# Gating and last rows on VectorE, a second PSUM bank for the scan's transposes, and decays and pool products written at other places

## The chip, the cores and the metric

The kernel runs on one core of a Trainium2 chip. Five engines work side by side, each through its own instructions in order: TensorE (PE; its weight loads are shown as PEld), VectorE (DVE), ScalarE (ACT), GpSimd (POOL) and SyncE (SP), which here only issues DMA transfers. ACT and POOL issue DMAs too, in line with their other work. [...] The metric is the device time of one execution in microseconds, the median of several runs.

## The reference

One layer over 512 latent tokens (and 256 context tokens as a prefix), 1024 wide, all in fp32:

```python
u = rmsnorm(h, g) * (1 + scale) + shift          # adaLN; shift, scale, gate from silu(c) @ ada_w + ada_b
z, xbc, dt, pool, q, k, v = split(u @ w_in)      # one input projection
y = ssd(xbc, dt, forward) + ssd(xbc, dt, backward) + d_skip * xs
ssd_out = rmsnorm(y * silu(z), ssd_norm_g)       # gate, then norm
pool_out = (window means of pool - pool) @ pool_w * pool_scale
na_out = neighbourhood attention(q, k, v, context k and v)
h = h + g1 * (concat(ssd_out, pool_out, na_out) @ w_out)
u = rmsnorm(h, norm2_g) * (1 + sc2) + sh2
h = h + g2 * peer_ffn(u)                         # 8 heads, 128 x 128 product keys, top 16 each
out = rmsnorm(h, final_g)
```

The SSD scan works in chunks of 128 tokens. Its decays are exponentials of sums of `dt * a` inside a chunk: to the chunk's end (en), over the whole chunk (to) and from its start (in), each for the forward and the backward direction. The expert part takes, for every token, 128 of 16384 experts; each expert is a row of `peer_u` and a row of `peer_v`.

## The kernel before

Matmuls of the large projections are done in three passes: an operand x is split into a rounded part (ACT copies it, line 175) and a remainder (mostly DVE subtracts, line 178), and `mm3` (lines 185 to 187) adds high times high, high times low and low times high. So each weight block needs a DMA on SP's queue, a copy on ACT and a subtraction on DVE before PE can use it. Weight blocks go through a few buffers (`ws`), so a block is split when PE has left the block that had its buffer.

The order of work comes from two sources. Inside `tc.manual_schedule()` every engine (or the engines that it names) takes its instructions in the order in which the program writes them. Elsewhere a planner orders the instructions of each engine, by the program's order and its own estimate of when operands are ready; `tc.keep_in_program_order` binds the instruction that it wraps. In both cases an engine that waits for an operand holds up all that is queued behind it on that engine.

The stages, in order:

1. *Input projection* (from about 20 to 232 us, planned from line 430 on). `projT` computes a block of 128 columns for all tokens into banks of `psG` (six). For the SSD columns (`cb` 0 to 11) a convolution and transposes follow. Between the projections the generator `ada_rest` is advanced by `next(ada)`, 17 times in all: it works out the second and third of three banks of the modulation. Each advance loads two 128 x 1024 pieces of `ada_w` and adds them, weighted, into `adac` on DVE (lines 478 and 480); after eight of them, at the ninth and at the seventeenth advance, line 484 sums `adac` over partitions on PE, line 487 adds the bias, line 489 stores the rows on SP's queue and line 492 transposes them. Then come four pool blocks: a projection, sums over windows on POOL (lines 626 to 633), and a 128 x 128 matmul in `pool_out` (line 613), which is put off by two blocks, so that the last two stand in the first two of four K projections. The V projection for the context follows.
2. *Scan* (to about 407, manual). A plan of 61 steps (`at(step, f, ...)`) lists what is issued in each; the same steps carry the projections of z, of V and of q (`z_mm`, `q_mm`) as other work for PE. PSUM: `psT` one bank, `psM` two, `psY` one, `psG2` four. Six `decay` calls stand ahead of the plan. For each chunk c the outputs are gathered in `ys[c]`: `o_add` multiplies on DVE and adds on POOL (lines 881 and 882), then `f_gate` multiplies by silu(z) on POOL (line 906), `f_square` squares on ACT, `f_norm` scales on DVE, `f_T` transposes 512 columns into the bank of `psT` (line 924), `f_out` empties it on DVE with the norm's gain (line 930), and `f_store` writes to `mix_d`. `f_T` and `f_out` occur twice for each chunk, one step apart.
3. *Attention and first half of the output projection* (to about 505, manual).
4. *Output projection and second norm* (to about 580; PE in program order, other engines planned in the first part). `out_end` scales an accumulator on DVE (line 1232), adds it to h (POOL for the first half, line 1233) and squares on ACT (line 1234); its buffer `otmp` has two copies. Two operations on `bcr` (lines 1247 and 1248, POOL) work out a gain row that the second norm of row block 3 reads.
5. *Queries, top 16 and routing* (to about 820) *and dense routing weights* (to about 1060).
6. *Experts* (to 1790). 128 steps; in each, a block of 128 experts' `peer_u` and `peer_v` for row blocks 0 to 2; row block 3 is done by gathering rows, in `accG`. The last three steps' `peer_v` products run by row block (`e_v(P - a, t)`), so that a row block can be ended while PE works on the next.
7. *The end.* For each row block: `f_mul` multiplies by the gate row and adds h (lines 1802 and 1803), `f_gain` multiplies by the final norm's gain (line 1815), `f_sq` squares on ACT, and `f_norm` takes the root and scales, half on ACT and half on DVE, or all on ACT. Additions and gains of row blocks 3, 0 and 1 run on POOL, those of 2 on DVE.

Of the kernel before, what the change touches and what calls it, by code (L numbers as in the profile page):

```python
# [148 lines left out]
def build(tc, A, out, dbg=None):  # L149
# [129 lines left out]
    an = si.tile([P, 2, NT, NH], F32, name="an")  # L279

# [185 lines left out]
    def ada_bank(bank, pool):  # L466

        adab = pool.tile([P, 512], F32, name="adab")
        nc.scalar.dma_start(adab, A["ada_b"][:, (bank - 1) * 512:bank * 512])
        part = pool.tile([P, 2048], F32, name="adac")  # L470
        for k in range(KB):
            n = (bank - 1) * KB + k
            for jj in range(2):
                w = xin[(2 * n + jj) % NT] if n < 12 else xin[3 + (2 * n + jj) % 3]
                nc.sync.dma_start(w, A["ada_w"][k * P:(k + 1) * P, (bank - 1) * 2048 + jj * 1024:(bank - 1) * 2048 + (jj + 1) * 1024])
                dst, ck = part[:, jj * 1024:(jj + 1) * 1024], cc[:, k, 0:1]
                if k:
                    tc.keep_in_program_order(V.scalar_tensor_tensor(dst, w, ck, dst, ALU.mult, ALU.add))
                else:
                    tc.keep_in_program_order(V.tensor_scalar(dst, w, ck, None, ALU.mult))  # L480
            yield None
# [6 lines left out]
        for j in range(4):  # L488
            nc.sync.dma_start(mod_d[bank - 1, j:j + 1, :], m[32 * j:32 * j + 1, :])
        pt = psT.tile([P, 4, P], F32, name="pt")  # L490
        for q in range(4):
            PE.transpose(pt[:, q, :], m[:, q * P:(q + 1) * P], ident)

        yield pt.rearrange("p m (j r) -> p j m r", r=32)

    def ada_rest():

        for r in ada_bank(1, ad1):
            if r is None:
                yield  # L500
            else:
                V.tensor_copy(jm(sh2T), r[:, 2:4, :, 0])
        for r in ada_bank(2, ad1):
            if r is None:
                yield
            else:
                V.scalar_tensor_tensor(jm(sc2T), r[:, 0:2, :, 0], 1.0, jm(n2g), ALU.add, ALU.mult)
# [131 lines left out]
    for b in range(4):  # L639
# [4 lines left out]
        if pend:  # L644
            pool_out(*pend.pop(0))
    tc.keep_in_program_order(S.activation(pl1.tile([P, 1], F32, name="warmx"), epsc, AF.Exp))
    accs = projC(V0)
    for t, acc in enumerate(accs):
        V.tensor_copy(vc[:, t, :], acc)
# [75 lines left out]
    for i in range(16):  # L725
        at(fs(4 * i), p_load, i + 2)
        at(fs(4 * i + 1), p_split, i + 1)
        for t in range(4):
            if i < 12:
                if i + t:  # L730
                    at(fs(4 * i + t), z_mm, i // 4, i % 4, t)
# [9 lines left out]

    af = an[:, 0].rearrange("p t h -> p (t h)")
    ab = an[:, 1].rearrange("p t h -> p (t h)")
    HC = NT * NH

    def decay(mask, mov, nm):
        ps = psM.tile([P, 512], F32, name="mm")
        PE.matmul(ps[:, :HC], mask, mov, start=True, stop=True)
        d = m1.tile([P, NT, NH], F32, name=nm)
        S.activation(d.rearrange("p t h -> p (t h)"), ps[:, :HC], AF.Exp)  # L750
        return d
    enF, enB = decay(SU, af, "enF"), decay(SL, ab, "enB")
    z_mm(0, 0, 0)
    toF, toB = decay(ONE, af, "toF"), decay(ONE, ab, "toB")
    inF, inB = decay(U_in, af, "inF"), decay(L_in, ab, "inB")
    V.tensor_tensor(enB, enB, dtn[:, 1], ALU.mult)
    V.tensor_tensor(enF, enF, dtn[:, 0], ALU.mult)
# [143 lines left out]
    def f_gate(c):  # L901
        if "yraw" in dbg:
            nc.sync.dma_start(dbg["yraw"][c * P:(c + 1) * P, :], ys[c])
        for g in range(2):
            gs, hs = half_of(g)
            G.tensor_tensor(ys[c][:, gs], ys[c][:, gs], zts[c, g], ALU.mult)
# [930 lines left out]
    with order:  # L1837
# [6 lines left out]
        for i in range(-6, P + 1):  # L1844
# [23 lines left out]
            if i == 64:  # L1868
                f_load()
            if i == P - 6:  # L1870
                h_load()
# [60 lines left out]
```

## Time and profile before

| | us |
|---|---|
| median of 3 runs (lowest, highest) | 1805.65 (1803.29, 1807.18) |
| the profiled execution | 1804.08 |
| its span, first to last instruction | 1802.0 |
| first decay matmul (scan) | 232.56 |
| first attention scores | 407.58 |
| last matmul starts | 1789.55 |

The span is what the trace shows; the profiled execution took 2.1 us more around it. In a timeline's row stand the start, the duration, the engine, the line of the program, the operation, its output and inputs by name, the shapes and the count; in brackets how long the engine had been idle and what it had waited for. "ACTq" and "SPq" are DMAs issued by ACT and SP. Several instructions of one line in direct sequence are merged into one row, whose duration is that of all.

### The profile page before, as it was taken

To read this page: it belongs to the slowest core of one execution; us is meant where nothing else is said; L and a number is where in the kernel's file an instruction comes from. 1 tells how busy PE (TensorE), PEld (TensorE's weight loads), DVE (VectorE), ACT (ScalarE), POOL (GpSimd) and SP (SyncE) were. 2 spreads that over 40 slices of the span, in tenths; PEclk is the share of its full clock that TensorE was granted. 3 is DMA by queue.
4 is the path that set the end of the run, shared out by engine and by line. 5 is a ranking of instruction groups with operands and counts; after the bars stand their busy time and mean duration, and the time that the engine had idled before them with its cause. 6 is when DMAs were issued, how large, how long until landed. Compare 5 with 4: busy or idle time off the path is not lost.

```text
span 1802.0 us, 26025 instructions
## 1 busy us (share of the span) xinstructions
PE 1755.1 (97%) x9527; PEld 1497.4 (83%) x9527; DVE 1400.1 (78%) x2606; ACT 842.8 (47%) x1497; POOL 406.2 (23%) x276
## 2 busy tenths in 40 slices
PE   6999999999999999999999999999999999999996
PEld 4787776666678889999999998888888888888885
DVE  5679467966635579898999978878878888888876
ACT  4433255456535333456677764434434444444443
POOL 1103410352224443310111121211111111111103
PEclk9999999999999999999999999999999999999999
DMA  9347432168333533576999989999999999999971
GB/s 358 104 144 253 146 90 65 57 211 274 111 106 118 172 112 116 156 266 218 342 342 345 354 307 398 403 353 340 362 344 349 338 396 348 360 349 339 371 242 49
DMA packets 192048, 455.40 MB, mean 253 GB/s; under 512 B 13704, under 2 KB 117384, under 8 KB 173968
## 3 DMA queue, kind: packets, MB, share of 16 engines
q1 hardware_dynamic: 147280, 259.79, 42.6%
q0 software_dynamic: 18576, 136.32, 19.8%
q10 hardware_dynamic: 26064, 57.62, 8.7%
q8 instruction: 75, 1.23, 0.3%
q14 instruction: 53, 0.43, 0.1%
HBM read 401.10 MB, written 54.67 MB: 253 GB/s over the span
## 4 chain that ended last, share of the span: by engine, by line
PE 80%; DVE 2%; ACT 2%; issue 1%; DMA 1%; POOL 1%; SPq 0%; ACTq 0%; POOLq 0%; DVEq 0%
PE pu L185 10%; PE pu L187 10%; PE pu L186 10%; PE pv L186 9%; PE pv L187 9%; PE pv L185 9%; PE acc L185 4%; PE acc L187 4%; PE acc L186 4%; PE mm L845 2%; PE gdps L1651 1%; PE gdps L1652 1%; PE sps L1047 1%; PE mm L787 1%; PE pt L1077 1%
## 5 line engine op out<-in xcount | busy, mean ns | idle before, releaser
L178 DVE TENSOR_TENSOR wl<-wraw,wh 128x1024 fp32r<-128x1024 f32 x294 | 368.1, 1264 | 110.2 <-ACT wh L175 108.1
L175 ACT ACTIVATE wh<-wraw 128x1024 fp32r<-128x1024 f32 x328 | 341.2, 1053 | 196.9 <-PE acc L186 70.7
L185 PE MATMUL pu<-u2h,wh 128*128 128x384 f32 x1024 | 349.7, 342 | 0.0
L186 PE MATMUL pu<-u2l,wh 128*128 128x384 f32 x1024 | 344.8, 337 | 0.8 <-DVE u2l L178 0.8
L187 PE MATMUL pu<-u2h,wl 128*128 128x384 f32 x1024 | 345.4, 337 | 0.0
L1590 POOL DMA_INDIRECT row<-in_peer_uv,idxG x128 | 156.6, 1223 | 804.8 <-DVE accG L1604 710.8
L186 PE MATMUL pv<-wl,wwh 128*128 128x512 f32 x768 | 300.7, 392 | 1.9 <-DVE wl L178 1.8
L185 PE MATMUL pv<-wh,wwh 128*128 128x512 f32 x768 | 301.2, 392 | 0.3 <-ACT wh L175 0.3
L187 PE MATMUL pv<-wh,wwl 128*128 128x512 f32 x768 | 300.9, 392 | 0.0
L186 PEld LDWEIGHTS pu<-u2l,wh 128*128 128x128 f32 x1024 | 192.5, 188 | 2.9 <-DVE u2l L178 1.1
L185 PEld LDWEIGHTS pu<-u2h,wh 128*128 128x128 f32 x1024 | 192.3, 188 | 1.8
L187 PEld LDWEIGHTS pu<-u2h,wl 128*128 128x128 f32 x1024 | 192.2, 188 | 0.7 <-DVE wl L178 0.6
L186 PEld LDWEIGHTS pv<-wl,wwh 128*128 128x128 f32 x768 | 144.2, 188 | 33.6 <-DVE wl L178 3.5
L187 PEld LDWEIGHTS pv<-wh,wwl 128*128 128x128 f32 x768 | 144.2, 188 | 32.2
L185 PEld LDWEIGHTS pv<-wh,wwh 128*128 128x128 f32 x768 | 144.3, 188 | 30.4 <-ACT wh L175 0.7
L1604 DVE SCALAR_TENSOR_TENSOR accG<-row,wG,accG 128x1024 f32<-128x1024 f32 x127 | 162.5, 1280 | 4.7 <-ACT wG L1599 3.4
L1595 DVE CUSTOM_DVE_ANT_0 row<-row,u2G 128x1024 f32<-128x1024 f32 x128 | 155.2, 1219 | 0.0
L175 ACT ACTIVATE wwh<-acl 128x384 fp32r<-128x384 f32 x86 | 45.2, 526 | 206.4 <-DVE acl L1763 134.3
L1654 ACT ACTIVATE stg<-gdps 128x512 f32<-128x512 f32 x96 | 101.5, 1170 | 19.7 <-PE gdps L1652 17.2
L178 POOL TENSOR_TENSOR wl<-wraw,wh 128x1024 fp32r<-128x1024 f32 x34 | 81.6, 2405 | 112.1 <-ACT wh L175 80.5
L1757 ACT ACTIVATE act<-pu 128x384 f32<-128x384 f32 x42 | 20.6, 491 | 162.0 <-PE pu L187 147.9
L1763 DVE TENSOR_TENSOR act<-act,gd 128x384 f32<-128x384 f32 x42 | 23.5, 559 | 87.0 <-ACT act L1757 87.0
(410 smaller groups left out, 3113.1 us busy)
## 6 DMA issues: line engine op xcount, KB each, us to landing
wraw<-in_peer_ut SPq DMA_DIRECT2D x128, 512.0 KB
wraw<-in_peer_uv SPq DMA_DIRECT2D x128, 512.0 KB
gd<-gd_d SPq DMA_DIRECT2D x15, 1536.0 KB
gd_d<-stg ACTq DMA_DIRECT2D x11, 2048.0 KB
wraw<-in_w_in SPq DMA_DIRECT2D x40, 512.0 KB
acl<-act_d SPq DMA_DIRECT2D x86, 192.0 KB
act_d<-act ACTq DMA_DIRECT2D x84, 192.0 KB
wraw<-in_w_out SPq DMA_DIRECT2D x16, 512.0 KB
```

Of the source, the lines that this page charges most:

```text
L175: S.activation(hi, full, AF.Copy)
L178: (eng or V).tensor_tensor(lo, full, hi.bitcast(F32), ALU.subtract)
L185: PE.matmul(ps, ah, bh, start=start, stop=False)
L186: PE.matmul(ps, ah, bl, start=False, stop=False)
L187: PE.matmul(ps, al, bh, start=False, stop=stop)
L845: PE.matmul(ps, m, ms[d].rearrange("p a b -> p (a b)"), start=d == 0, stop=d == 1)
L1590: G.indirect_dma_start(out=rows[k], out_offset=None, in_=A["peer_uv"], in_offset=bass.IndirectOffsetOnAxis(ap=idxG[:, k:k + 1], axis=0))
L1595: V.tensor_tensor_reduce(row[:, 0:D], row[:, 0:D], u2G, 1.0, 0.0, ALU.mult, ALU.add, actG[:, k:k + 1])
L1604: V.scalar_tensor_tensor(accG, row[:, D:2 * D], wG[:, k:k + 1], accG, ALU.mult, ALU.add)
L1654: S.activation(stg[:, :, t0:t0 + 4].rearrange("p a t -> p t a"), ps, AF.Copy, scale=1.0 / GSCALE)
L1757: S.activation(ac[a], pu[:, :TD], AF.Gelu)
L1763: V.tensor_tensor(xq, xq, gds.pop(a), ALU.mult)
```

## The change

- The six decay tiles are allocated with the scan's inputs. Their matmuls and exponentials, bound to program order, stand between the K and the V projections, in two banks of `psG`; the products with `dtn` follow them. The `z_mm(0, 0, 0)` that stood between them is in the plan's step 0. An exponential that only loaded ACT's table (`warmx`) is left out.
- The generator is cut into `ada_sum` (one load-and-add), `ada_row` (lines 484 to 489) and `ada_col` (the transposes and what follows). Bank 1's row comes with the tenth advance, its transposes with the eleventh; bank 2's with the seventeenth and an eighteenth, after the V projection's matmuls. `adac` has two buffers.
- `pool_out` for the last two pool blocks stands after the second and the third K projection, instead of after the first and the second.
- `f_gate` multiplies on DVE.
- `f_T` writes its second half (`q4` 1) into `psY`'s bank.
- The two `bcr` operations are bound to program order.
- The end: h is loaded two steps earlier for row block 3; all additions run on DVE; there is no `f_gain`: `f_norm` is one fused DVE operation per half, (h times 1/rms) times gain, and each half is stored by SP and by ACT. Roots and reciprocals are issued apart. Row block 0's last products come one group earlier.

```diff
-        for k in range(KB):
-            n = (bank - 1) * KB + k
...
+    def ada_rest():
+        for n in range(16):
+            ada_sum(1 + n // KB, n % KB)
+            if n == 9:
+                ada_row(1)
+            if n == 10:
+                ada_col(1)
+            yield
+        ada_row(2)
+        yield
+        ada_col(2)
...
-        if pend:
+        if b and pend:
             pool_out(*pend.pop(0))
...
-    tc.keep_in_program_order(S.activation(pl1.tile([P, 1], F32, name="warmx"), epsc, AF.Exp))
+    HC = NT * NH
+    def decays(specs):
+        ps = psG.tile([P, 512], F32, name="acc")
+        for i, (mask, d, _) in enumerate(specs):
+            tc.keep_in_program_order(PE.matmul(ps[:, i * HC:(i + 1) * HC], mask, an[:, d].rearrange("p t h -> p (t h)"), start=True, stop=True))
+        for i, (_, _, t) in enumerate(specs):
+            tc.keep_in_program_order(S.activation(t.rearrange("p t h -> p (t h)"), ps[:, i * HC:(i + 1) * HC], AF.Exp))
+    decays([(SU, 0, enF), (SL, 1, enB), (ONE, 0, toF)])
+    decays([(ONE, 1, toB), (U_in, 0, inF), (L_in, 1, inB)])
+    for t, d in ((enB, 1), (enF, 0)):
+        V.tensor_tensor(t, t, dtn[:, d], ALU.mult)
     accs = projC(V0)
+    next(ada, None)
...
-            G.tensor_tensor(ys[c][:, gs], ys[c][:, gs], zts[c, g], ALU.mult)
+            V.tensor_tensor(ys[c][:, gs], ys[c][:, gs], zts[c, g], ALU.mult)
...
-        pt = psT.tile([P, 4, P], F32, name="pt")
+        pt = psY.tile([P, 512], F32, name="yd").rearrange("p (a b) -> p a b", a=4) if q4 else psT.tile([P, 4, P], F32, name="pt")
...
-            G.tensor_tensor(bcr, bcr, n2row, ALU.mult)
-            G.tensor_tensor(bcr, bcr, n2row, ALU.add)
+            tc.keep_in_program_order(G.tensor_tensor(bcr, bcr, n2row, ALU.mult))
+            tc.keep_in_program_order(G.tensor_tensor(bcr, bcr, n2row, ALU.add))
...
-        (V if t == 2 else G).tensor_tensor(hx[t][:, hs], sq[:, hs], hx[t][:, hs], ALU.add)
+        V.tensor_tensor(hx[t][:, hs], sq[:, hs], hx[t][:, hs], ALU.add)
...
     def f_norm(t):
         y = sqs[t][:, D:2 * D]
+        for hf in range(2):
+            hs = slice(hf * 512, (hf + 1) * 512)
+            V.scalar_tensor_tensor(y[:, hs], hx[t][:, hs], fss[t][:, 1:2], fgr[:, hs], ALU.mult, ALU.mult)
+            (nc.sync, nc.scalar)[hf].dma_start(out[t * P:(t + 1) * P, hs], y[:, hs])
...
-        for a, t in ((3, 0), (2, 0), (3, 1), (1, 0), (2, 1), (1, 1)):
+        for a, t in ((3, 0), (2, 0), (1, 0), (3, 1), (2, 1), (1, 1)):
             e_v(P - a, t)
             if a == 1:
                 f_mul(t, 0)
+                f_sq(t, 0)
                 f_mul(t, 1)
+                f_sq(t, 1)
+                if t == 0:
+                    f_rec(3)
+                    f_norm(3)
                 else:
-                    f_norm(3)
+                    f_rstd(0)
         for hf in range(2):
             for a in range(P - 3, P):
                 e_v(a, 2, (hf,))
+            f_mul(2, hf)
+            f_sq(2, hf)
+            f_rec(0) if hf == 0 else f_rstd(1)
         f_norm(0)
+        f_rec(1)
+        f_rstd(2)
+        f_norm(1)
+        f_rec(2)
         f_norm(2)
```

More of the change, by code (lines that the diff above doesn't have):

```diff
@@ L279, in build @@
     an = si.tile([P, 2, NT, NH], F32, name="an")
+    enF, enB, toF, toB, inF, inB = (si.tile([P, NT, NH], F32, name=nm) for nm in ("enF", "enB", "toF", "toB", "inF", "inB"))
     gp = Pools()
@@ L464, in build, with ada_sum, ada_row @@
     ad1 = adp.sb("ad1")
-    def ada_bank(bank, pool):
-        adab = pool.tile([P, 512], F32, name="adab")
-        nc.scalar.dma_start(adab, A["ada_b"][:, (bank - 1) * 512:bank * 512])
-        part = pool.tile([P, 2048], F32, name="adac")
-        for k in range(KB):
-            n = (bank - 1) * KB + k
[L473 to L481, printed above, removed]
+    adac = {}
+    def ada_sum(bank, k):
+        if k == 0:
+            adac[bank] = ad1.tile([P, 2048], F32, name="adac", bufs=2)
+        part = adac[bank]
+        n = (bank - 1) * KB + k
+        for jj in range(2):
+            w = xin[(2 * n + jj) % NT] if n < 12 else xin[3 + (2 * n + jj) % 3]
+            nc.sync.dma_start(w, A["ada_w"][k * P:(k + 1) * P, (bank - 1) * 2048 + jj * 1024:(bank - 1) * 2048 + (jj + 1) * 1024])
+            dst, ck = part[:, jj * 1024:(jj + 1) * 1024], cc[:, k, 0:1]
+            if k:
+                tc.keep_in_program_order(V.scalar_tensor_tensor(dst, w, ck, dst, ALU.mult, ALU.add))
+            else:
+                tc.keep_in_program_order(V.tensor_scalar(dst, w, ck, None, ALU.mult))
+    def ada_row(bank):
+        adab = ad1.tile([P, 512], F32, name="adab")
+        nc.scalar.dma_start(adab, A["ada_b"][:, (bank - 1) * 512:bank * 512])
+        part = adac.pop(bank)
         ps = psG.tile([P, 512], F32, name="acc")
@@ L729, in build @@
             if i < 12:
-                if i + t:
-                    at(fs(4 * i + t), z_mm, i // 4, i % 4, t)
+                at(fs(4 * i + t), z_mm, i // 4, i % 4, t)
                 if i % 4 == 3:
@@ L740, in build @@
                        v_d.rearrange("(r c) d -> r c d", c=64)[:, KCOL[g]:KCOL[g] + 32, :]))
[L742 to L757, printed above, removed]
     def hbc(ap):
@@ L1780, in f_load, with h_load @@
         row_bc(g2r, 2, 2, nc.sync)
-    hx = {}
-    def h_load():
-        hr = gls[1].tile([P, NQ, 8 * TQ], F32, name="gd", bufs=2).rearrange("p q t -> p (q t)")
-        for t in (3, 0, 1, 2):
+    hx, stds = {}, {}
+    def h_load(ts):
+        if 3 not in ts:
+            hr = gls[1].tile([P, NQ, 8 * TQ], F32, name="gd", bufs=2).rearrange("p q t -> p (q t)")
+        for t in ts:
             hx[t] = u2G if t == 3 else hr[:, t * D:(t + 1) * D]
```

64 lines of the change are left out of this document (17 added, 47 removed).

## The prediction

> **What bounds the kernel now.** I read the page's first lines, then the table of stretches, then what TensorE (PE) waited for, then the timelines around those waits.
>
> ```profile
> span 1802.0 us, 26025 instructions
> PE 1755.1 (97%) x9527; PEld 1497.4 (83%) x9527; DVE 1400.1 (78%) x2606; ACT 842.8 (47%) x1497; POOL 406.2 (23%) x276
> ```
>
> PE is busy 97%: an edit can win only what PE stands idle, what it runs at half clock, and the end after its last matmul. The stretches (us, then PE, PEld, DVE, ACT, POOL busy with counts, granted clock, DMA share, GB/s) show where these lie:
>
> ```profile
> 147.00:197.00 50.00, 46.85 (x219) 35.65 (x220) 48.82 (x36) 13.39 (x20) 31.66 (x24) 1.00 0.84 269
> 384.70:387.80 3.10, 0.00 (x0) 0.00 (x0) 2.52 (x5) 1.52 (x5) 0.95 (x2) 1.00 0.51 184
> 387.80:391.20 3.40, 3.36 (x8) 2.25 (x9) 1.77 (x5) 0.29 (x1) 0.71 (x1) 0.50 0.16 48
> 580.00:1770.00 1190.00, 1189.61 (x6551) 1073.34 (x6550) 995.57 (x1965) 564.23 (x925) 239.42 (x166) 1.00 0.84 304
> ```
>
> From 580 to 1770 PE idles 0.4 us, so whatever is won ahead of 580 arrives at the end undiminished. Near the scan's end PE stands still for 3.1 us and then runs 3.4 us at clock 0.50. The waits of PE (total, times, longest), the last row from the stretch 1770 to 1802:
>
> ```profile
> PE pt L924 <- DVE y L930: 3.2, 1, 3.2
> PE acc L484 <- DVE adac L478: 2.2, 1, 2.2
> PE acc L185 <- DVE otmp L1232: 1.7, 1, 1.7
> PE acc L613 <- POOL pa L633: 1.5, 1, 1.5
> PE acc L613 <- POOL pb L633: 0.9, 1, 0.9
> PE pv L186 <- DVE wl L178: 1.5, 2, 0.8
> ```
>
> Each is in code that the diff edits. They sum to 11.0 us; the half clock and the end come on top.
>
> **The change part by part.**
>
> *Modulation sums and pool products (120 to 220).* Line 484's matmuls of bank 1 move from the ninth advance of the generator to the tenth, behind the first pool projection; their four transposes to the eleventh. Line 613's last two products move one K projection back.
>
> ```profile
> 156.33 0.69 DVE L487 TENSOR_TENSOR mod<-acc,adab 128x512 f32<-128x512 f32 x1 [1.14 <-PE acc L484]
> L478 DVE SCALAR_TENSOR_TENSOR adac<-qT,cc,adac 128x1024 f32<-128x1024 f32 x8 | 16.4, 2071 | 0.0
> 178.29 2.31 DVE L178 TENSOR_TENSOR wl<-wraw,wh 128x1024 fp32r<-128x1024 f32 x1
> 180.13 0.80 PE L401 MATMUL acc<-uh,wh 128*128 128x512 f32 x1
> 187.85 2.14 POOL L633 TENSOR_TENSOR pb<-pb,pl 128x512 f32<-128x512 f32 x1
> 189.81 0.58 ACT L641 ACTIVATE kT<-acc 128x512 f32<-128x512 f32 x1
> 199.67 1.27 POOL L633 TENSOR_TENSOR pa<-pa,pl 128x512 f32<-128x512 f32 x1
> 200.15 0.58 ACT L641 ACTIVATE kT<-acc 128x512 f32<-128x512 f32 x1
> ```
>
> POOL ends the late operands at 190.0 and 200.9; K projections are copied out at 189.8 and 200.2, some 10 us apart, so a product one projection later finds its operand ready with over 8 us to spare: 0.9 + 1.5 = 2.4 us. The 2.2 us at line 484 go too, since DVE gets the time of a projection (24 matmuls, 0.23 us apart, 5.6 us). But DVE is full here (48.8 of 50 us), and next late is its split for the first K projection: it ends at 180.6, and PE, which starts that projection at 180.13, needs it 0.7 us on. DVE itself gets only its 1.14 us wait back and the 0.69 us addition moved later within the full stretch. So of 2.2 I count 1.6: **4.0 us** together (0.5 if DVE sets the whole stretch, 4.6 if nothing does). On SP's queue the four stores of line 489 now stand behind two more weight loads; behind them wait later w_in loads, which are prefetched.
>
> *Decays.* The same six small matmuls and exponentials run before the V projection instead of at the scan's start. They sum to nothing, as PE does them in both places (three rows of the length below, 2.1 us, is the loss if PE were idle there before). What may go is the first one's wait:
>
> ```profile
> 232.56 0.69 PE L748 MATMUL mm<-an,cst 128*128 128x96 f32 x4 [0.89 <-DVE vc L649]
> ```
>
> The scan then starts with a projection matmul in another PSUM bank. Whether that bank is also held by the copies of line 649 the trace cannot show: -2.1 to 0.9; the lower end needs a PE that is idle before the V projection, which no wait shows: **0.5**.
>
> *Second bank and gate on DVE (the scan's end).*
>
> ```profile
> 362.12 0.68 DVE L852 TENSOR_TENSOR t<-t,t 128x512 f32<-128x512 f32 x1
> 363.48 1.65 POOL L882 TENSOR_TENSOR xsn<-xsn,ytmp 128x512 f32<-128x512 f32 x1 [4.16 <-DVE ytmp L881]
> 363.92 1.76 DVE L857 TENSOR_TENSOR t<-t,ee 128x512 f32<-128x512 f32 x1
> 381.58 3.51 POOL L906 TENSOR_TENSOR xsn<-xsn,t 128x512 f32<-128x512 f32 x2
> 381.96 1.99 DVE L178 TENSOR_TENSOR wl<-wraw,wh 128x1024 fp32r<-128x1024 f32 x1 [1.69 <-ACT wh L175]
> 383.88 1.23 DVE L916 TENSOR_TENSOR ysq<-ysq 128x1 f32<-128x1 f32 x1
> 384.29 0.40 PE L187 MATMUL acc<-uh,wl 128*128 128x512 f32 x1
> 387.01 0.68 DVE L930 TENSOR_TENSOR y<-pt,colv 128x512 f32<-128x512 f32 x1
> 387.84 1.09 PE L924 MATMUL pt<-cst,y 128*128 128x128 f32 x4 [3.15 <-DVE y L930]
> 389.57 0.15 DVE L916 TENSOR_TENSOR ysq<-ysq 128x1 f32<-128x1 f32 x1
> ```
>
> PE's second group of transposes waits until DVE has emptied the one bank (387.69). In psY's bank it can go at 384.69, as that bank's last reader stands at step 45 of the plan and the transposes at 50. This removes 3.1 us and the half clock's loss (3.4 x 0.5 = 1.7), 4.8. [...]
>
> Next late is the third group, which needs the first bank again: PE arrives there after four transposes, two scan matmuls and six projection matmuls (0.4 + 0.9 + 1.4), at 387.4. DVE's emptying, now at 387.69, loses POOL's interference (twice 1.23 - 0.15, and 1.99 - 1.23, 2.9) and gains four gates before it (4 x 0.68 = 2.7): about 387.5. Even, so I count **4.3** (bounds -1.3, rival B, and 4.8). POOL's eight gates leave; behind them waited its additions.
>
> *Output projection.*
>
> ```profile
> 513.55 3.27 POOL L1248 TENSOR_TENSOR bcr<-bcr,xn 128x1024 f32<-128x1024 f32 x1
> 516.77 2.51 POOL L1233 TENSOR_TENSOR h<-h,otmp 128x512 f32<-128x512 f32 x2
> 518.85 0.69 DVE L1232 TENSOR_TENSOR otmp<-acc,g1r 128x512 f32<-128x512 f32 x1 [3.70 <-ACT otmp L1234]
> ```
>
> POOL does the two bcr operations first; the four additions to h wait, with them ACT's squares, the two otmp buffers, and PE's accumulator. In program order they come after the additions, and bcr is not read until the last row block's norm. **1.7** (0 to 1.7).
>
> *The end.*
>
> ```profile
> 1774.90 2.21 DVE L178 TENSOR_TENSOR wl<-wraw,wh 128x1024 fp32r<-128x1024 f32 x1
> 1780.27 1.23 DVE L178 TENSOR_TENSOR wl<-wraw,wh 128x1024 fp32r<-128x1024 f32 x1 [0.39 <-ACT wh L175]
> 1787.90 0.69 DVE L1802 TENSOR_TENSOR row<-pv,g2r 128x512 f32<-128x512 f32 x1 [1.40 <-PE pv L187]
> 1789.55 0.40 PE L187 MATMUL pv<-wh,wwl 128*128 128x512 f32 x1
> 1792.24 0.69 DVE L1803 TENSOR_TENSOR gd<-row,gd 128x512 f32<-128x512 f32 x1
> 1797.08 0.72 ACT L1821 ACTIVATE row<-row,rstd 128x512 f32<-128x512 f32 x1 [0.29 <-DVE rstd L257]
> ```
>
> Without POOL beside it, and with block 3's products two iterations earlier, the split that took 2.21 takes 1.23 and starts sooner; PE's 1.5 us of waits go, though the last weights are now needed one 1.4 us group earlier. PE ends at 1788.5. Behind it on DVE: a product and an addition (1.38), three norms of two fused operations (no row has one of this width; I take the addition's 0.69, 4.14 in all; half the 2.07 of line 478, 1.04, is the upper end, 2.1 more), and some 0.6 of one-column work: 6.1, so 1794.6. Before, from the last operation's end (1797.80) to the span's end were 4.2; with the same 4.2 the end is 1798.8: **3.3 us** (1.2 with the upper price; 4.5 if less output is left to write behind the last operation, since the row blocks now end one after the other).
>
> *Sum:* 4.0 + 0.5 + 4.3 + 1.7 + 3.3 = 13.8. The profiled execution took 1804.08 (its span 1802.0 and 2.1 around it) and would take 1790.3; the runs' median is 1805.65, 1.6 above it, and gives **1791.9**. The ends of the terms, all at once, are 1805.65 + 1.7 = 1807.4 (0.5 - 2.1 - 1.3 + 0 + 1.2 = -1.7) and 1805.65 - 16.5 = 1789.2.
>
> **The rivals.**
>
> *A, DVE sets the projection stage.* For it: 48.8 of 50 us busy; against: the waits show PE held there by DVE once, at line 484. First term 0.5 instead of 4.0: 1795.4.
>
> *B, the gates collide with POOL's additions.* An operation with two SBUF inputs took 1.76 instead of 0.68 beside such an addition. Four gates at 1.76 put DVE's emptying at 391.8; PE, waiting from 387.4, loses 4.4 and the clock again, 1.7: the third term becomes 4.8 - 6.1 = -1.3 and the time 1797.5. Against it: in program order each gate follows its block's additions, and few others are then due. [...]
>
> *C, slower: the transposes of bank 1 stand behind DVE's queue.* DVE takes its work in order, and the addition at line 487 that feeds them now falls into the full stretch. If the planner, which placed line 484 2.2 us too early, puts it behind all twelve half-sums left (12 x 2.07 = 24.8), PE stands 24.8 less one projection, 19.2 us, at the transposes, and SP's queue with it at line 489: 1811.1. From ten half-sums on (20.7 - 5.6 = 15.1, against the 13.8 won) the kernel is slower. Against: before, the addition ran right after its matmuls.
>
> *D, no change.* The planner's other order on DVE and ACT gives back most gains as new waits: for it, 78% busy DVE; against, PE's own order is written out by hand from 231 on. About 1804.
>
> **How the numbers follow.** Forecast 0.58, A 0.16, B 0.12, D 0.07, C 0.07. A measurement of this kernel can tell about 0.2% (3.6 us) from no change. Forecast, A and B are faster, less 0.01 for a B at its worst: 0.85; D and that, 0.08; C 0.07. The range runs from 1787, the upper ends less the runs' own scatter (the lowest run is 2.4 below the median), to 1800, B with that scatter on the other side; D and C are left out.
>
> **What would show it.** After: no wait of PE at lines 484, 613, 924 and at otmp's multiplication; clock 1.00 through the scan's end; POOL's h additions ahead of bcr; the span's end 8 to 10 us after the last matmul instead of 12.05. A wait at the transposes of line 492, or a new one on line 178 near 180, would be C or A; one at the third group of transposes, B. The prediction is wrong if these waits are gone and the scan and the attention still start when they did.

## The result and the profile after

The changed kernel takes **1794.2 us** (median of 6 runs, 1793.35 to 1795.82) against 1805.0 us for the kernel before (6 runs): ratio 0.9941, 95% interval 0.993 to 0.9952. The forecast was 1791.9, with a range of 1787 to 1800. The kernel is faster by 10.8 us where 13.8 were summed up. Line numbers below are those of the changed kernel; in the projection stage they lie 1 to 26 higher than before, from the scan's body on 8 higher.

The page of the changed kernel, first lines:

```profile
span 1791.6 us, 25999 instructions
PE 1751.3 (98%) x9527; PEld 1497.4 (84%) x9527; DVE 1402.1 (78%) x2624; ACT 838.5 (47%) x1491; POOL 376.7 (21%) x256
```

To see where the time went, the starts of the same matmuls are compared in both traces: one in the projections, the first state product of the scan, the first scores of the attention, the first of the experts' `peer_u` matmuls. In the timeline (start, length) of the kernel before:

```profile
103.91 0.40 PE L401 MATMUL acc<-uh,wh 128*128 128x512 f32 x1
239.87 1.02 PE L787 MATMUL mm<-xd,Bn 128*128 128x512 f32 x2
407.58 0.70 PE L1047 MATMUL sps<-kT,qT 64*128 64x256 f32 x4 [0.69 <-ACT qT L707]
570.71 0.34 PE L185 MATMUL pu<-u2h,wh 128*128 128x384 f32 x1
```

and of the changed kernel, with its last matmul:

```profile
104.14 0.39 PE L402 MATMUL acc<-uh,wh 128*128 128x512 f32 x1
241.25 1.02 PE L795 MATMUL mm<-xd,Bn 128*128 128x512 f32 x2
404.48 0.70 PE L1055 MATMUL sps<-kT,qT 64*128 64x256 f32 x4 [0.69 <-ACT qT L733]
565.62 0.34 PE L185 MATMUL pu<-u2h,wh 128*128 128x384 f32 x1
1782.01 0.40 PE L187 MATMUL pv<-wh,wwl 128*128 128x512 f32 x1
```

The differences of these starts give each stage's length. The span is 10.4 us shorter, and it divides so:

| stage | before | after | difference | forecast |
|---|---|---|---|---|
| to the matmul at 104 | 103.91 | 104.14 | +0.2 | 0 |
| P: from there to the scan's first state product | 135.96 | 137.11 | **+1.1** | -4.5 (4.0 and 0.5) |
| S: scan, to the attention's first scores | 167.71 | 163.23 | -4.5 | -4.3 |
| O: attention, output projection, queries, to the first `pu` | 163.13 | 161.14 | -2.0 | -1.7 |
| E: experts, to the end of the last matmul | 1219.24 | 1216.78 | -2.5 | -1.5 |
| T: behind the last matmul | 12.05 | 9.18 | -2.9 | -1.8 |

Four stages came as forecast or better. One, P, went the other way: its waits of before are gone, and it is still longer. The granted clock and the busy time by stretch (length, PE, PEld, DVE, ACT, POOL busy, clock, DMA share, GB/s) show it:

```profile
147.00:197.00 50.00, 43.33 (x200) 33.95 (x200) 42.01 (x35) 13.02 (x20) 27.09 (x23) 0.93 0.75 237
164.60:171.30 6.70, 0.08 (x1) 0.00 (x0) 5.77 (x6) 1.54 (x2) 3.92 (x2) 0.84 0.81 282
171.40:174.80 3.40, 3.40 (x6) 2.08 (x7) 2.99 (x2) 0.69 (x1) 3.32 (x4) 0.50 0.97 320
371.00:403.80 32.80, 32.67 (x148) 23.93 (x146) 26.87 (x42) 17.21 (x35) 9.33 (x6) 1.00 0.74 238
```

PE was busy 46.85 of the 50 us from 147 to 197 before; now it is 43.33, with a hole of 6.7 us and a half clock that lasts from 169.1 to 175.9. PE works in the last 4.6 us of that, so the half clock costs it some 2.3 us, half of 4.6. The last row is the scan's end: PE stands still for 0.13 of 32.8 us, at full clock. The hole in the timeline of the changed kernel, the engines around it (an entry in brackets is the idle time before the instruction and what ended it; ACTq are the DMA issues in ACT's queue):

```profile
159.10 0.51 ACTq L631 DMA_DIRECT2D pcnt<-in_pcnt  x1
167.30 1.79 POOL L645 TENSOR_TENSOR pb<-pa,pcnt 128x512 f32<-128x512 f32 x1 [5.84 <-DMA pcnt<-in_pcnt]
169.12 0.36 ACTq L631 DMA_DIRECT2D pcnt<-in_pcnt  x1
169.17 2.13 POOL L646 TENSOR_TENSOR pb<-pb,pl 128x512 f32<-128x512 f32 x1
169.53 0.60 ACT L637 ACTIVATE pl<-acc 128x512 f32<-128x512 f32 x1 [9.28 <-POOL pb L645]
171.10 1.28 DVE L178 TENSOR_TENSOR wl<-wraw,wh 128x1024 fp32r<-128x1024 f32 x1 [0.93 <-ACT wh L175]
171.36 2.08 PE L626 MATMUL acc<-pb,pw 128*128 128x512 f32 x2 [6.67 <-POOL pb L646]
```

PE waits 6.67 us at line 626 for the operand of the first pool product. POOL could not make it sooner: its window counts `pcnt`, issued at 159.1, arrived at 167.3. The same product in the kernel before, with POOL's two operations ahead of it:

```profile
166.61 2.18 POOL L632 TENSOR_TENSOR pb<-pa,pcnt 128x512 f32<-128x512 f32 x1 [2.41 <-DMA pcnt<-in_pcnt]
168.86 2.17 POOL L633 TENSOR_TENSOR pb<-pb,pl 128x512 f32<-128x512 f32 x1
172.79 1.02 PE L613 MATMUL acc<-pb,pw 128*128 128x512 f32 x2
```

There the counts were late too, and the operand was ready at 171.0, hardly sooner. The product found it ready, because it stood behind the 24 projection matmuls of pool block 2. In the changed kernel it stands two matmuls into them, some 5 us of PE earlier. The diff does not touch this product (it moves the last two); the planner put it there, as it orders anew whatever is not bound. The fourth `pcnt` issue in ACT's queue waits for a buffer that POOL frees at 169.1, and holds ACT for 9.28 us (4.92 before). Behind it stands the copy that block 3's split needs, the one at 171.10; block 2's split was done at 166.7 (starts of the blocks' matmuls: block 1 at 158.0, block 2 at 164.0).

The other places that the prediction named, in the changed kernel. At the scan's end the second group of transposes goes into its own bank, and the third follows without a pause:

```profile
386.30 0.60 PE L932 MATMUL yd<-cst,y 128*128 128x128 f32 x4
389.03 0.63 PE L932 MATMUL pt<-cst,y 128*128 128x128 f32 x4
```

In the output projection POOL adds to h first, then comes `bcr`; DVE's `otmp` multiplication waits 1.34 us instead of 3.70, and PE not at all:

```profile
511.65 0.69 DVE L1240 TENSOR_TENSOR otmp<-acc,g1r 128x512 f32<-128x512 f32 x1 [1.34 <-ACT otmp L1242]
512.42 2.56 POOL L1241 TENSOR_TENSOR h<-h,otmp 128x512 f32<-128x512 f32 x2 [0.30 <-DVE otmp L1240]
514.95 2.40 POOL L1255 TENSOR_TENSOR bcr<-bcr,xn 128x1024 f32<-128x1024 f32 x1
```

And the last operation on DVE, behind PE's end at 1782.40:

```profile
1786.88 1.41 DVE L1829 SCALAR_TENSOR_TENSOR row<-gd,fss,fgr 128x512 f32<-128x512 f32 x2
```

### The profile page after: what moved, and what is told of

Its sections match the earlier page's. It is cut to its first block, busy times and chain, and to the rows that moved or that the text cites. A ratio compares the mean times of both kernels' runs of the same rounds, so it can differ in the third digit from the quotient of the medians.

```text
span 1791.6 us, 25999 instructions
## 1 busy us (share of the span) xinstructions
PE 1751.3 (98%) x9527; PEld 1497.4 (84%) x9527; DVE 1402.1 (78%) x2624; ACT 838.5 (47%) x1491; POOL 376.7 (21%) x256
## 4 chain that ended last, share of the span: by engine, by line
PE 91%; DMA 3%; DVE 3%; ACT 2%; issue 1%; POOL 1%; SPq 0%; ACTq 0%; DVEq 0%; POOLq 0%
PE pu L185 10%; PE pu L187 10%; PE pu L186 10%; PE pv L187 10%; PE pv L185 10%; PE pv L186 10%; PE acc L185 5%; PE acc L187 5%; PE acc L186 5%; PE mm L853 2%; PE acc L404 1%; PE acc L402 1%; PE acc L406 1%; PE gdps L1659 1%; PE gdps L1660 1%; PE sps L1055 1%
```

## The experiments

All are edits of the changed kernel. The table has the median, the ratio to runs of the kernel before taken at the same time (medians 1804.4 to 1805.05) with its interval, and the stage lengths of the profiled execution, read as above. A profiled execution is one run: P and, by estimate, O also contain what a half clock costs there, and that differs from profile to profile (in P it lasts 6.8 us in the changed kernel, 10.2 in e7_bcr; last section).

| kernel | median us | ratio (95%) | P | S | O | E | T |
|---|---|---|---|---|---|---|---|
| before | 1805.0 | 1 | 135.96 | 167.71 | 163.13 | 1219.24 | 12.05 |
| changed | 1794.20 | 0.9941 (0.9930 to 0.9952) | 137.11 | 163.23 | 161.14 | 1216.78 | 9.18 |
| e1_pcnt | 1789.73 | 0.9916 (0.9903 to 0.9930) | 132.72 | 163.73 | 161.12 | 1216.86 | 9.24 |
| e2_order | 1788.69 | 0.9906 (0.9891 to 0.9921) | 131.95 | 163.24 | 162.64 | 1216.36 | 9.19 |
| e3_both | 1792.10 | 0.9927 (0.9914 to 0.9941) | 134.19 | 163.23 | 162.92 | 1216.72 | 9.25 |
| e4_projold | 1793.79 | 0.9943 (0.9930 to 0.9957) | 136.88 | 163.28 | 161.11 | 1216.74 | 9.18 |
| e5_onebank | 1795.59 | 0.9947 (0.9933 to 0.9960) | 137.60 | 166.06 | 161.13 | 1216.65 | 9.17 |
| e6_poolgate | 1794.97 | 0.9947 (0.9933 to 0.9960) | 137.76 | 163.77 | 161.07 | 1216.75 | 9.18 |
| e7_bcr | 1797.55 | 0.9963 (0.9952 to 0.9974) | 138.14 | 163.24 | 163.06 | 1216.92 | 9.18 |
| e8_splits | 1798.93 | 0.9972 (0.9960 to 0.9984) | 141.05 | 163.22 | 161.07 | 1216.29 | 9.17 |
| e9_endpool | 1793.59 | 0.9943 (0.9929 to 0.9957) | 137.32 | 163.22 | 161.07 | 1216.61 | 9.23 |
| e10_later | 1789.39 | 0.9909 (0.9892 to 0.9925) | 132.53 | 163.24 | 161.08 | 1216.37 | 9.19 |
| e11_later_pcnt | **1786.20** | 0.9891 (0.9874 to 0.9908) | 128.89 | 163.51 | 161.13 | 1216.46 | 9.25 |
| e13_evorder | 1794.71 | 0.9945 (0.9931 to 0.9959) | 137.04 | 163.23 | 162.66 | 1216.59 | 9.85 |

### The projection stage: four runs on the first theory

**Window counts early** (the first two blocks' into a buffer of their own ahead of the convolutions, the other two into two buffers):

```diff
-    adac = {}
+    adac, pcnt01 = {}, ad1.tile([P, 2, SEQ], F32, name="pcnt01")
+    nc.scalar.dma_start(pcnt01, A["pcnt"][:, :2 * SEQ].rearrange("p (b s) -> p b s", b=2))
...
-        pcnt = pl2.tile([P, SEQ], F32, name="pcnt")
-        nc.scalar.dma_start(pcnt, A["pcnt"][:, b * SEQ:(b + 1) * SEQ])
+        pcnt = pcnt01[:, b, :] if b < 2 else pl2.tile([P, SEQ], F32, name="pcnt", bufs=2)
+        b < 2 or nc.scalar.dma_start(pcnt, A["pcnt"][:, b * SEQ:(b + 1) * SEQ])
```

> The changed kernel, with the window counts of the first two pool blocks loaded before the convolutions into a buffer of their own and those of the other two into two buffers of their own, so that POOL does not wait for them and no issue on ACT's queue waits for a buffer that POOL frees. The first pool product still stands two matmuls into block 2. Theory 1 (the 6.67 us wait at line 626 and the 6.8 us of half clock behind it come from the late window counts): POOL's two operations of block 0 end near 165.5 instead of 171.3, the wait at line 626 falls under 1.5 us, the first scan-state matmul comes 5 to 6 us earlier, near 235.5, and the kernel takes about 1788.5 us (1787.5 to 1790). Rival 1 (the weight splits on DVE set this stage, rival A of the prediction): the wait moves to weight matmuls that wait for DVE near 166 to 181, and the kernel stays at 1793 to 1795.

Measured 1789.73. PE's waits in this stretch (timeline of this kernel):

```profile
166.61 1.10 PE L626 MATMUL acc<-pb,pw 128*128 128x512 f32 x2 [1.83 <-DMA pw<-in_pool_w]
169.16 0.50 PE L187 MATMUL acc<-uh,wl 128*128 128x512 f32 x1 [0.99 <-DVE wl L178]
175.63 0.50 PE L187 MATMUL acc<-uh,wl 128*128 128x512 f32 x1 [1.18 <-DVE wl L178]
```

6.67 us became 1.83, where theory 1 had said less than 1.5, and what ends it now is another transfer, the pool weights `pw`, issued in the same place as the counts were. Two waits for split weights from DVE, 2.2 us together, stand behind it. So the late counts made most of the wait, as theory 1 said, but rival 1's wait was there too, covered by the longer one. There is no half clock: P is 4.4 us shorter, and the stage now lies 3.2 below the kernel before.

**Products kept in place** (the edit binds all four pool products; the first is the one that had moved):

```diff
-        PE.matmul(pp, pw[:, b, :], src[:, 8:520], start=True, stop=True)
+        tc.keep_in_program_order(PE.matmul(pp, pw[:, b, :], src[:, 8:520], start=True, stop=True))
```

> The changed kernel, with the pool products kept where the program has them, so that the first one follows all 24 matmuls of pool block 2 instead of standing two matmuls into it. Rival 2 (the place of that product alone makes the wait): the wait goes and the kernel takes about 1788. Theory 1: ACT is still held 9.28 us by the issue that waits for a buffer, the split weights of block 2 are ready only at 172.4 (171.10 + 1.28), so the wait moves from line 626 to the weight matmuls of block 2, and the kernel takes 1792.5 to 1795.

Measured 1788.69: rival 2's time, against theory 1. The wait did move to the weight matmuls of block 2, but it is a third of the 6.67 us and ends at 168.4, not at 172.4. Theory 1 had taken the split at 171.10 for block 2's; it is block 3's. ACT is held 9.49 us in this kernel too, and PE waits for nothing that stands behind that. ACT, DVE and PE in the timeline of this kernel:

```profile
158.61 1.06 ACT L175 ACTIVATE wh<-wraw 128x1024 fp32r<-128x1024 f32 x1 [3.37 <-issue]
164.71 1.27 DVE L480 SCALAR_TENSOR_TENSOR adac<-kT,cc,adac 128x1024 f32<-128x1024 f32 x1
165.91 1.28 DVE L480 SCALAR_TENSOR_TENSOR adac<-qT,cc,adac 128x1024 f32<-128x1024 f32 x1
167.18 1.21 DVE L178 TENSOR_TENSOR wl<-wraw,wh 128x1024 fp32r<-128x1024 f32 x1
168.44 0.50 PE L187 MATMUL acc<-uh,wl 128*128 128x512 f32 x1 [2.12 <-DVE wl L178]
```

The split that PE waits for could have started at 159.7, when ACT had made the high part. It stands in DVE's queue behind the half-sums of the modulation, the last two of them the eleventh step's, and starts 7.5 us later. So the place of the product and the late counts both have to be there for the 6.67 us; taking either away wins 4.4 to 5.2 us of P. Behind them comes DVE.

**Both together:** the two edits above.

> Both edits: window counts early and in buffers of their own, and the pool products kept in program order. Theory 1: like the early window counts alone or up to 1.5 us faster, 1787 to 1789, with no wait over 1 us at line 626. Rival 1 (DVE sets the stage): 1793 to 1795 again.

Measured 1792.10, slower than either alone. That fits neither number exactly; the wait is rival 1's. This kernel's timeline:

```profile
164.33 2.13 POOL L646 TENSOR_TENSOR pb<-pb,pl 128x512 f32<-128x512 f32 x1
165.26 2.28 DVE L480 SCALAR_TENSOR_TENSOR adac<-qT,cc,adac 128x1024 f32<-128x1024 f32 x1
169.60 0.56 PE L187 MATMUL acc<-uh,wl 128*128 128x512 f32 x1 [4.39 <-DVE wl L178]
```

The same two operations in the changed kernel, where neither has the other beside it:

```profile
164.26 1.27 DVE L480 SCALAR_TENSOR_TENSOR adac<-qT,cc,adac 128x1024 f32<-128x1024 f32 x1
176.75 1.29 POOL L646 TENSOR_TENSOR pa<-pa,pl 128x512 f32<-128x512 f32 x1
```

With early counts POOL multiplies by them at 162.1 instead of at 167.3, and DVE's last two half-sums and the split behind them take 1.74, 2.28 and 2.00 us, where e2_order has 1.27, 1.28 and 1.21. The wait for that split grows from 2.12 to 4.39. In the rows, the half-sum and POOL's subtraction take 2.28 and 2.13 us with the other engine at work beside them, and 1.27 and 1.29 without, 2.56 one after the other.

**Projection edits undone** (bank 1's sum and transposes in one step ahead of bank 2, bank 2's in one step, pool products shifted back):

```diff
-            if n == 9:
-                ada_row(1)
-            if n == 10:
-                ada_col(1)
+            if n == KB:
+                ada_row(1)
+                ada_col(1)
...
-        if b and pend:
+        if pend:
```

> The changed kernel with the projection stage's edits undone: adaptive-norm bank 1 is summed into rows and transposed in one step ahead of bank 2's first products, as before, bank 2 in one step behind the key blocks, and the pool products are shifted back by a key block. Decays, second bank, gates, output projection and end stay changed. Theory 1 (these edits lost about what they won, 1.4 us net with the scan start): 1792 to 1793.5, with the three waits of the kernel before back (adaptive-norm matmuls and late pool products). Rival 3 (the prediction's first term of 4.0 us was won, and something else was lost): 1797 to 1798.

Measured 1793.79, as theory 1 said. The waits of before are back, four instead of three:

```profile
PE acc L491 <- DVE adac L480: 2.2, 1, 2.2
PE pt L502 <- DVE mod L494: 1.7, 1, 1.7
PE acc L626 <- POOL pa L646: 1.5, 1, 1.5
PE acc L626 <- POOL pb L646: 1.0, 1, 1.0
```

They sum to 6.3 us, against 6.67 and a half clock in the changed kernel: P is 136.88 against 137.11. The projection edits as they stand are worth nothing. The fourth wait, at bank 2's transposes, is new against the kernel before, where nine matmuls of the V projection stood ahead of them; what this kernel still has changed in the stage is above all the place of the decays, and its P is 0.9 us longer than before.

### The projection stage: DVE's queue

The second theory: once the product is out of the way, the stage is held by splits that stand behind half-sums on DVE. Two ways were tried to get the split that PE waited for ahead. The expectations below call it block 1's, and the half-sums the tenth step's; counted by the matmuls, it is block 2's, and they are the eleventh step's.

**Splits, sums and products all bound to program order:**

```diff
+    kept = [False]
     def split(hi, lo, full, eng=None, lows=None):
...
-            (eng or V).tensor_tensor(lo, full, hi.bitcast(F32), ALU.subtract)
+            r = (eng or V).tensor_tensor(lo, full, hi.bitcast(F32), ALU.subtract)
+            kept[0] and tc.keep_in_program_order(r)
```

with `kept[0]` true for the pool and key blocks, and the matmuls of lines 626, 491 and 502 wrapped as in e2_order.

> The changed kernel with the pool products, the modulation sums' matmuls and transposes and DVE's weight splits of the pool and key blocks all kept in program order, so that the split of block 1 stands ahead of the tenth step's two half-sums on DVE's queue, not behind them. Theory (after the product, the order on DVE's queue makes the rest of the stage's loss: with the product kept in place PE still waited 2.12 us for a split that was ready to start 7 us earlier): that wait and the 3.4 us of half clock behind it go, no wait over 0.7 us between 150 and 230, and 1784 to 1786.5. Rival (rival A of the prediction, DVE has no room in this stretch whatever the order): the wait moves to line 493, line 504 or a later split, and the kernel stays at 1787.5 to 1790.5.

Measured 1798.93, worse than either said. The waits of PE:

```profile
PE acc L189 <- DVE wl L179: 10.4, 3, 7.4
```

The binding did not do what it was meant to: in program order the split of block 2 stands behind the eleventh step's half-sums, and PE waited 1.40 us for it again. It also put the splits of blocks 0 and 1 behind the ninth and the tenth step's, where the planner had drawn them ahead: PE waited 7.39 and 1.58 us for those. The run says nothing against the theory, nor for it. It says that a whole chain bound to program order loses what the planner had won elsewhere.

**One step of sums moved** to where DVE idles. In the changed kernel DVE has idle stretches of 8 us between 204 and 222; none are left from 158 to 170.

```diff
         px, _ = projT(A["w_in"][:, PL0 + b * P:PL0 + (b + 1) * P], False)
-        next(ada, None)
+        b and next(ada, None)
...
         S.activation(kT[:, b, SEQ:], pc[:, :CTX], AF.Copy, scale=-1.0)
-        next(ada, None)
+        [next(ada, None) for _ in range(1 + (b == 2))]
```

> The changed kernel with one step of the modulation sums moved: pool block 0 advances the generator no more, and the third key block advances it twice, so that two half-sums leave DVE's full stretch behind 160 for the stretch behind 200, where DVE idles 8 us at a time; everything behind them (bank 1's row, its transposes) comes one pool block later too. The planner now puts the first pool product behind block 2's projection by itself. Theory (DVE has no room from 158 to 176: the product kept in place still left a 2.12 us wait for a split queued behind half-sums): the split of block 1 starts by 165, no wait over 0.7 us from 150 to 230, no half clock there, 1785 to 1787. Rival (the waits in this stretch come from the planner's order, and DVE's load does not matter): another wait of 2 us or more for a split or a product, 1788 to 1791.

Measured 1789.39, the rival's time, and of the two waits that the rival named the one for a product. POOL and PE in this kernel:

```profile
168.56 2.27 POOL L645 TENSOR_TENSOR pb<-pa,pcnt 128x512 f32<-128x512 f32 x1 [6.43 <-DMA pcnt<-in_pcnt]
173.09 1.13 PE L626 MATMUL acc<-pb,pw 128*128 128x512 f32 x2 [2.75 <-POOL pb L646]
```

DVE's splits are in time: no wait over 0.3 us for one between 150 and 230, so DVE's load did matter, against the rival. Block 2 then runs through, PE reaches the product (which the planner now has behind block 2's matmuls by itself) at 170.3, and the counts are still late. The wait for DVE and the wait for the counts cover one another.

**All of it taken away**: the moved step, the early counts, and the products kept.

> The same moved step, and the early window counts of e1 with it, and the pool products kept in program order. Theory (early counts hurt in e3 only because POOL then worked beside DVE while a split was queued behind half-sums): with room on DVE the two edits agree, no wait over 0.7 us from 150 to 230, within 1.5 us of the moved step alone, 1784.5 to 1787.5. Rival (POOL beside DVE, 2.0 to 2.3 us for a split or half-sum instead of 1.2 to 1.3, is enough for a new wait): a wait of 1 to 4 us for a split between 160 and 180, 1788 to 1792.

Measured **1786.20** (1784.58 to 1788.19), 0.9891 of the kernel before: the fastest median of all, and what the theory said. The interval overlaps e2_order's; the stage length, 3.1 us shorter than there, decides. PE's only wait over 0.3 us from 150 to 228, and the stretch of 50 us:

```profile
166.30 0.50 PE L187 MATMUL acc<-uh,wl 128*128 128x512 f32 x1 [0.63 <-DVE wl L178]
147.00:197.00 50.00, 49.37 (x243) 39.29 (x242) 49.28 (x36) 15.91 (x24) 35.24 (x26) 1.00 0.84 260
```

PE is busy 49.37 of 50 us, and so is DVE, 49.28: in this stretch PE has 0.6 us left to win. P is 128.89, 8.2 below the changed kernel and 7.1 below the kernel before.

### The scan's end

**One bank for all transposes, gates on DVE:**

```diff
-        pt = psY.tile([P, 512], F32, name="yd").rearrange("p (a b) -> p a b", a=4) if q4 else psT.tile([P, 4, P], F32, name="pt")
+        pt = psT.tile([P, 4, P], F32, name="pt")
```

> The changed kernel with one PSUM bank for both groups of transposes at the scan's end, as before; the gates stay on DVE. Theory (the second bank is what removes the wait): PE waits again 2.5 to 4 us at the second group for DVE's emptying, and runs 3.4 us at clock 0.50 behind it, so the attention starts 4 to 6 us later and the kernel takes 1798.5 to 1800. Rival (the gates' move off POOL, which slowed DVE before, is what won the 4.5 us): DVE empties the bank in time, the wait is under 1.5 us with no half clock, and the kernel takes 1794 to 1796.

**Two banks, gates on POOL:**

```diff
-            V.tensor_tensor(ys[c][:, gs], ys[c][:, gs], zts[c, g], ALU.mult)
+            G.tensor_tensor(ys[c][:, gs], ys[c][:, gs], zts[c, g], ALU.mult)
```

> The changed kernel with the eight gates back on POOL and the second bank kept. Theory (the second bank is enough): no wait over 0.5 us at the second group, at most 1 us at the third, and 1793.5 to 1795.5. Rival (the gates' place matters as much): POOL's gates stand behind its additions and slow DVE's operations, PE waits 1.5 to 4 us at the second or third group or at the last norm, and the kernel takes 1796 to 1799.

The medians, 1795.59 (in the range of e5_onebank's rival) and 1794.97, lie within the scatter of the changed kernel, so the stage lengths have to decide. S is 167.71 with neither edit, 166.06 with the gates alone, 163.77 with the bank alone, 163.23 with both: 1.65, 3.94 and 4.48. The theory holds: the bank takes the wait away (0.5 us is left of it without the gates), and behind it the gates add 0.5. Of the 1.65 without the bank, 0.67 is a shorter wait, since DVE empties the bank sooner (PE's waits with the gates alone, and the stretch behind that wait with its clock):

```profile
PE pt L932 <- DVE y L938: 2.5, 1, 2.5
390.20:393.60 3.40, 3.39 (x17) 2.59 (x18) 2.28 (x6) 0.74 (x2) 0.77 (x1) 1.00 0.24 75
```

The wait is 2.48 instead of 3.15 us, and the clock does not fall behind it, which leaves some 1.0 of the 1.65 to the half clock that didn't come. Whether the gates are to be thanked for that is not shown, as pauses of about this length were followed by a half clock in some kernels (2.12 and 2.75 us) and not in another (2.17; last section). The theory had the wait right, at its low end, and the half clock wrong.

### The output projection

```diff
-            tc.keep_in_program_order(G.tensor_tensor(bcr, bcr, n2row, ALU.mult))
-            tc.keep_in_program_order(G.tensor_tensor(bcr, bcr, n2row, ALU.add))
+            G.tensor_tensor(bcr, bcr, n2row, ALU.mult)
+            G.tensor_tensor(bcr, bcr, n2row, ALU.add)
```

> The changed kernel with the two operations on bcr left to the planner again, which puts them ahead of POOL's four additions to h, as before. Theory (the prediction's fourth term): PE waits 1.7 us for the multiplication into otmp again, nothing else changes, and the kernel takes 1795.5 to 1796.5. Rival (in the changed kernel bcr costs as much in its new place, where it runs beside DVE's splits, 2.97 and 3.06 us): within 0.7 us of the changed kernel, 1793.5 to 1794.9.

Measured 1797.55, 3.4 above the changed kernel. The wait is back in its place:

```profile
518.22 0.50 PE L185 MATMUL acc<-wh,mBh 128*128 128x512 f32 x1 [1.62 <-DVE otmp L1240]
```

O is 163.06, 1.9 longer. The other 1.4 us of the median are not the edit's by anything shown: in the profiled execution, 3.9 above the changed kernel's, P is 1.0 longer (wait 7.36 at line 626, and 10.2 us of half clock instead of 6.8) and the start up to the matmul at 104 is 0.75 longer, both in stages that the edit doesn't touch, and the runs scatter from 1794.85 to 1801.3. The theory's term is right; its total left out how much the first pool wait varies.

### The end

**Additions of row blocks 0, 1 and 3 back on POOL:**

```diff
-        V.tensor_tensor(hx[t][:, hs], sq[:, hs], hx[t][:, hs], ALU.add)
+        (V if t == 2 else G).tensor_tensor(hx[t][:, hs], sq[:, hs], hx[t][:, hs], ALU.add)
```

> The changed kernel with the end's additions of row blocks 0, 1 and 3 to h back on POOL (six operations), all else kept. Theory (POOL beside DVE is part of what held the end: DVE's splits beside it took 2.21 us against 1.23): PE's waits for split weights among the last 40 matmuls come back in part, 0.5 to 1 us, the additions take 1.3 to 3.3 us instead of 0.69 and the last norms wait for them, 1 to 3 us in all: 1795.5 to 1798. Rival (the end's gain comes from the order and the fused norms alone): within 0.7 us of the changed kernel, 1793.5 to 1795.

Measured 1793.59, E 1216.61 and T 9.23: no difference, so the rival holds. Four of POOL's six additions now lie behind the last split; the first two run from 1753.72 to 1756.97, where a split of `wwl` is due (in the trace of before one took 0.93 us beside POOL's work, at 1773.95, and 0.56 without), and E shows no wait of PE for it.

**The last six groups of matmuls in the order of before:**

```diff
-        for a, t in ((3, 0), (2, 0), (1, 0), (3, 1), (2, 1), (1, 1)):
+        for a, t in ((3, 0), (2, 0), (3, 1), (1, 0), (2, 1), (1, 1)):
```

> The changed kernel with the last six groups of matmuls in the order of the kernel before, so that the last expert's split weights are needed one group of 1.4 us later and row block 0 is complete one group later. Theory (the end was won by the fused norms and by what left POOL, the order of the groups does nothing): within 0.7 us of the changed kernel, 1793.5 to 1794.9. Rival (row block 0, done one group earlier, is what lets its norm stand ahead): 1795 to 1796.

Measured 1794.71, in the theory's range. Yet T is 9.85 instead of 9.18 with E the same, so by this one profile the order is worth some 0.7 us. What is left of the end's 5.3 must lie in the fused norms, in the multiplications by the gain that left POOL (two of them, 3.84 us, ran beside the split of 2.21 in the trace of before) and in block 3's earlier products; no run took these apart.

## Why the prediction was right and where it was wrong

The forecast of faster held, and the time lay 2.3 us above the forecast, within its range. The sum was not right in its parts: one term was wrong in sign, and others were larger than counted. That the total came so close is partly luck.

**Projection stage and scan start: 4.5 counted, -1.1 measured.** This is the step that failed. The prediction worked out the instructions that the diff moves, and each of these did what it said: no wait at the sums of bank 1, none at the last two pool products. It took the first product, which the diff leaves alone, as staying where it was. The planner put it 22 matmuls sooner, ahead of POOL's operand, and 6.67 us and a half clock took the place of 4.5 us of waits. Binding the pool products turned the stage from 1.1 worse than before to 4.0 better. The 6.67 and the 2.3 us of the half clock are 4.5 more than the waits that went, and P is only 1.1 longer: the matmuls themselves now follow one another more closely. Bank 1's sums are one part of that, one group of 1.0 us where the planner of before had made two of 1.0 each; the rest was not traced. One sign that the prediction named for being wrong half came: its waits are gone, and the scan starts 1.4 us later than before. Why the planner chose that place is open; its estimates are not in a trace. Of the 0.5 us counted for the decays, 0.3 came at the wait that it was counted for: the wait of 0.89 at the scan's start is 0.61 in the changed kernel, now for `sc2T` from bank 2's transposes. With the old order of the modulation (e4_projold) the wait for `vc` stayed, 0.98, and the stage came out 0.9 longer than before.

The prediction did not mention ACT's queue in this stage, where a DMA issue that waits for a buffer held ACT for 9.28 us. In e2_order it was held 9.49 us, and PE waited for nothing behind it; in the changed kernel the split that it delayed, block 3's, was done at 172.4, and PE did not wait for that either.

**Rival A** (DVE sets this stage) forecast 1795.4, closer to the measured time than the forecast was, but not for the reason that acted: in the changed kernel PE waits for POOL. Its mechanism is real one layer down. With the product bound, the 2.16 us at line 484 came back as 2.12 us for a split; with POOL beside it, as 4.39; and the stage gave up the last 3 us only when a step of DVE's sums was moved out of it as well. So the wait counted at line 484 was moved by the edit as made, and came back at the next operand from DVE once the product was out of the way.

**Scan's end: 4.3 counted, 4.5 measured.** The mechanism is as told: the bank, with the gates even. Rival B's wait at the third group did not come.

**Output projection: 1.7 counted, 2.0 measured**, and e7_bcr shows that it is the order of `bcr`.

**The end: 3.3 counted, 5.3 measured,** above the upper bound of 4.5; PE's waits went and DVE's work behind PE came as told, e9_endpool shows no part for the additions that left POOL, and two sizes were low. Ahead of the last matmul the prediction took 1.5 from the two waits of 0.8 in the table of waits; E shortened by 2.5: a third wait, 0.28 for ACT, was too short to be in that list, and the matmuls beside each wait stood 0.1 to 0.3 us farther apart. Behind it, DVE's work was 6.1 counted and 5.9 measured (1788.29 - 1782.40, with the fused operation at 0.70, the lower price), and the time from the last operation to the span's end 3.3 instead of 4.2, the 4.5 case named for it.

**Rivals C and D** fell. C's premise came true in part: the addition at line 494 starts at 162.47, 4.4 us behind the end of its matmuls, after four of DVE's operations. The transposes, put off by one projection, reach it at 163.6 and do not wait. D's mechanism, a new order by the planner that turns gains into waits, acted in stage P, on PE's own queue; elsewhere the gains were not given back.

**The two sums.** 13.8 counted; by stages the measured differences are 1.1 lost, and 4.5, 2.0, 2.5 and 2.9 won, less 0.2 in the stage ahead: 10.4 by the span, 10.7 by the profiled executions (1804.08 - 1793.35). The sizes that were too low, the end's two above all, hid not quite half of a wrong sign.

## What to carry to other kernels

Where a planner orders part of the work, an edit moves more than it names: bind the instructions whose place the saving rests on, or read the order of the new program before summing, above all for instructions with late operands. A wait that is taken away uncovers the next one behind it, so ask for every late operand of a stage which other operand would be late right after it; here two causes covered one another, and either edit alone left behind a third to a half of what the stage gained with all three edits. In the rows here, a half-sum on DVE and a subtraction on POOL, both with two inputs in SBUF, took 2.28 and 2.13 us beside work of the other engine, against 1.27 and 1.29 without it, so making POOL earlier spent DVE's time.

## What the runs showed of the hardware

**Half clock after pauses shorter than its own length.** The stretches of half clock read in the scan and the projections are 3.4 us long (the kernel before at 387.8, e2_order, e10_later), 6.8 (the changed kernel at 169.1) or 10.2 (e7_bcr at 168.0); in the two long pauses (6.67 us in the changed kernel, 7.36 in e7_bcr) they begin while PE still stands. A pause of 2.12 us in e2_order was followed by one (the wait itself, then the stretch behind it):

```profile
166.30:168.44 2.14, 0.02 (x1) 0.00 (x0) 2.09 (x3) 0.00 (x0) 0.00 (x0) 1.00 1.04 409
168.80:172.20 3.40, 3.40 (x10) 2.62 (x9) 2.57 (x2) 0.86 (x2) 2.52 (x2) 0.51 0.38 119
```

A pause of 2.17 us in e4_projold was not, nor was the 2.48 us of e5_onebank above:

```profile
154.60:160.00 5.40, 5.40 (x24) 2.89 (x25) 4.25 (x6) 0.00 (x0) 0.00 (x0) 1.00 0.77 259
```

In e10_later 2.75 us was followed by one, too. So 3.4 us at half clock came behind pauses of 2.12, 2.75 and 3.15 us (the last in the kernel before), and none came behind 2.17 and 2.48; what decides it, no run here shows. As an estimate from these, a pause of 2 to 3 us is worth itself or itself and 1.7 us, half of 3.4.

**The price of such a stretch is as large as some edits.** In e2_order, e3_both and e13_evorder O is 162.64, 162.92 and 162.66 us against 161.14 in the changed kernel, 1.5 to 1.8 longer with nothing edited in it. That is about what one stretch of 3.4 us costs (1.7, the estimate above); that it was one is not shown, though the mean granted clock of e13_evorder's profiled execution is 0.994, against 0.996 for the changed kernel. Differences below 2 us were read from stage lengths for that reason, not from the medians.
